# Differential probabilities turned through DRAM, in a one-layer hybrid attention kernel on one core

## The chip, the core and the metric

The kernel runs on one core of a Trainium2 chip. Five engines work side by side, each in the order of its own queue: TensorE (PE, with its weight load PEld), VectorE (DVE), ScalarE (ACT), GpSimd (POOL) and SyncE (SP), which here only issues DMAs. Engines wait for each other by semaphores. The metric is the device time of one execution in microseconds, lower is better.

## What is computed

One transformer layer over 256 latent tokens and 256 context tokens, width 2048, all in float32. A combined input projection feeds two kinds of attention: grouped-query attention (branch A, 16 heads of 128) and differential attention (branch B, 8 heads, each with two 64-wide halves). The part that the change concerns is branch B: two softmaxes are subtracted, and the difference is multiplied with the values.

```python
def diff_attn(q, k, v, lam, lam_init, subln_g):
    s = jnp.einsum('bnhid,bmhid->bhinm', q, k).astype(jnp.float32) * (dh ** -0.5)
    p = jax.nn.softmax(s, axis=-1)
    a = (p[:, :, 0] - lam * p[:, :, 1]).astype(v.dtype)
    o = jnp.einsum('bhnm,bmhe->bnhe', a, v)
    o = rms_norm(o, subln_g) * (1 - lam_init)
...
x_new = x + m_lat[2] * merge_branches(oa, ob, ga, gb, w_br_a, w_br_b, w_out)
x_new = swiglu_sublayer(x_new, ...)
```

Around it stand the modulated norms, two gates, the output projection and a gated feed-forward part with 5632 hidden columns.

## The kernel before

**Matmuls in three passes.** Each weight block of 256 rows and 512 columns is loaded by SP into a buffer `wraw` (7 of them), rounded by ACT into `whi` (L227), and the rest `wlo` is made by DVE (L229). TensorE then does three matmuls for each product: high by high, high by low, low by high (`mm3`, L233 to L235). One such block serves two row tiles of 128 tokens and two row blocks, so 12 matmuls. There are three buffers of `whi` and three of `wlo`.

**Fill pieces.** `project` (L635) runs one projection of 512 columns as a generator: each step is one weight block, 12 matmuls. `filler` (L822) chains the query groups, the gate projections and the B output projection into a stream of such pieces. Attention is cut into units that are woven into this stream: 16 units of branch B (8 heads by 2 row tiles), then 16 of branch A.

**A unit of branch B.** `front` (L713) issues six score matmuls (`s`, L734), two softmaxes (`mx` on DVE, `p` on ACT), and joins the two into one probability tile `p` of 128 queries by 512 keys (L740, L741). `back` (L746) is a generator that `on` advances by one step twice in each later unit: the tile is turned by four TensorE transposes into PSUM (`ptp`, L758) and copied by ACT to `pT` (L764); then four matmuls with the values make `o` (L779); ACT squares it, DVE scales the sum (`rstdo`, L119), POOL takes the power (L120), and DVE writes `on` (L784); two steps later `on` is turned (`otp`, L788).

**Helpers with a delay.** `after(n, fn)` runs `fn` when n weight blocks of the projections have gone by. A query group is normed by `norm_rope` (L456) for both row tiles at once, right when its projection ends, and turned 5 and 6 blocks later; its units may begin 7 blocks after the end.

**Elsewhere.** The feed-forward part already turns its activations through DRAM (`turned`, L1032): a DVE transpose within 32 by 32 blocks into `fpart`, one POOL DMA to `turn_d`, and four POOL DMAs back into `fturn`, in an order that completes the turn. In the output projection, `out_evac` (L947) makes the new rows `xn` and stores them, and `scaled` (L967) multiplies them in place by a row of scales; the call stands one block into the next column group.

**What sets the order.** The program is written in the order that these generators give. A scheduler then places the instructions on each engine's queue. `tc.issue_after(x)` keeps an instruction behind x. Buffers set the rest: the tag `p` has four tiles, `tp` and `s` two PSUM tiles each.

```python
870        pr = front(br, u)
873        on()
874        take(fill, 2)
875        on()
876        while pieces[0] + 0.5 < goal and next(fill, fill) is not fill:
877            pass
878        work.append(back(br, u, pr))
```

## Time and profile before

| What | us |
|---|---|
| Median of three runs | 1710.86 (1710.63 to 1713.24) |
| The profiled execution, whole | 1709.15 |
| Its span, first to last instruction | 1707.4 |
| TensorE busy | 1682.6 (99%) |
| VectorE busy | 1147.5 (67%) |
| ScalarE busy | 769.8 (45%) |
| GpSimd busy | 202.6 (12%) |

The granted TensorE clock is 0.998 of full speed over the span. The units of branch B lie between about 376 and 618 us, those of branch A between about 600 and 800 us, the output projection between about 890 and 985 us, and the feed-forward part behind it. In the views that follow, "x" is a count of instructions, "ns" the duration of one, and "landing" the time from the issue of a DMA until its data has arrived. Row labels read: line, engine, operation, output tile, then its inputs. L120 or L229 are lines of the kernel file as it was before.

### The profile page before, as it was taken

To read this page: it belongs to the slowest core of one execution; us is meant where nothing else is said; L and a number is where in the kernel's file an instruction comes from. 1 tells how busy PE (TensorE), PEld (TensorE's weight loads), DVE (VectorE), ACT (ScalarE), POOL (GpSimd) and SP (SyncE) were. 2 spreads that over 40 slices of the span, in tenths; PEclk is the share of its full clock that TensorE was granted. 3 is DMA by queue.
4 is the path that set the end of the run, shared out by engine and by line. 5 is a ranking of instruction groups with operands and counts; after the bars stand their busy time and mean duration, and the time that the engine had idled before them with its cause. 6 is when DMAs were issued, how large, how long until landed. Compare 5 with 4: busy or idle time off the path is not lost.

```text
span 1707.4 us, 21517 instructions
## 1 busy us (share of the span) xinstructions
PE 1682.6 (99%) x7889; PEld 1355.0 (79%) x7889; DVE 1147.5 (67%) x1459; ACT 769.8 (45%) x1045; POOL 202.6 (12%) x296
## 2 busy tenths in 40 slices
PE   6999999999999999999999999999999999999999
PEld 4677778887887788878888788888888888888887
DVE  5765779788788879796666755566666666554554
ACT  4222223245656566667544544444444444433332
POOL 1200002011031110011111101111111111100000
PEclk9999999999999999999999999999999999999999
DMA  7888785678756677777777857788888888766662
GB/s 286 304 296 279 264 333 163 216 253 260 250 181 221 218 239 242 233 239 239 246 276 237 291 173 218 227 270 269 263 268 271 263 274 258 235 219 192 218 207 90
DMA packets 181291, 413.15 MB, mean 242 GB/s; under 512 B 15008, under 2 KB 16240, under 8 KB 180928
## 3 DMA queue, kind: packets, MB, share of 16 engines
q1 hardware_dynamic: 168912, 374.23, 66.9%
q0 software_dynamic: 12272, 37.53, 7.3%
q8 instruction: 62, 1.02, 0.2%
q14 instruction: 45, 0.37, 0.1%
HBM read 395.42 MB, written 16.29 MB: 241 GB/s over the span
## 4 chain that ended last, share of the span: by engine, by line
PE 91%; DVE 5%; issue 1%; DMA 1%; ACT 1%; POOL 0%; SPq 0%; DVEq 0%; ACTq 0%; POOLq 0%
PE mm L233 28%; PE mm L234 27%; PE mm L235 27%; PE ada L290 2%; PE ptp L758 1%; DVE wlo L229 1%; PE o L779 1%; PE s L734 1%; DVE nr L479 0%; ACT whi L227 0%; DMA tok<-in_x_dram 0%; DVE ss L464 0%; DVE sq L475 0%; DVE mx L686 0%; DMA x_d<-xn 0%
## 5 line engine op out<-in xcount | busy, mean ns | idle before, releaser
L229 DVE TENSOR_TENSOR wlo<-wraw,whi 128x1024 fp32r<-128x1024 f32 x497 | 605.9, 1220 | 417.0 <-ACT whi L227 416.2
L227 ACT CAST whi<-wraw 128x1024 fp32r<-128x1024 f32 x498 | 523.3, 1052 | 745.6 <-PE mm L235 626.5
L234 PE MATMUL mm<-wlo,hT 128*128 128x512 f32 x684 | 266.4, 389 | 0.0
L235 PE MATMUL mm<-whi,hT 128*128 128x512 f32 x684 | 266.3, 389 | 0.0
L233 PE MATMUL mm<-whi,hT 128*128 128x512 f32 x684 | 266.3, 389 | 0.0
L233 PE MATMUL mm<-whi,xT 128*128 128x512 f32 x630 | 251.5, 403 | 0.7 <-ACT xT L334 0.7
L234 PE MATMUL mm<-wlo,xT 128*128 128x512 f32 x630 | 247.4, 393 | 0.9 <-DVE wlo L229 0.9
L235 PE MATMUL mm<-whi,xT 128*128 128x512 f32 x630 | 246.3, 391 | 0.0
L431 DVE SCALAR_TENSOR_TENSOR ada<-wada,vt,ada 128x1024 f32<-128x1024 f32 x120 | 152.2, 1279 | 0.0
L234 PEld LDWEIGHTS mm<-wlo,hT 128*128 128x128 f32 x684 | 128.5, 188 | 26.9 <-DVE wlo L229 0.2
L235 PEld LDWEIGHTS mm<-whi,hT 128*128 128x128 f32 x684 | 128.4, 188 | 26.8
L233 PEld LDWEIGHTS mm<-whi,hT 128*128 128x128 f32 x684 | 128.5, 188 | 26.3
L233 PEld LDWEIGHTS mm<-whi,xT 128*128 128x128 f32 x630 | 117.8, 188 | 38.1 <-issue 12.3
L234 PEld LDWEIGHTS mm<-wlo,xT 128*128 128x128 f32 x630 | 118.6, 188 | 25.9 <-DVE wlo L229 2.1
L235 PEld LDWEIGHTS mm<-whi,xT 128*128 128x128 f32 x630 | 118.3, 188 | 25.1
L233 PE MATMUL mm<-whi,fT 128*128 128x512 f32 x354 | 137.6, 389 | 0.5 <-DVE y L1077 0.5
L235 PE MATMUL mm<-whi,fT 128*128 128x512 f32 x354 | 137.4, 388 | 0.0
L234 PE MATMUL mm<-wlo,fT 128*128 128x512 f32 x354 | 137.4, 388 | 0.0
L233 PEld LDWEIGHTS mm<-whi,fT 128*128 128x128 f32 x354 | 66.5, 188 | 15.3 <-issue 0.8
L235 PEld LDWEIGHTS mm<-whi,fT 128*128 128x128 f32 x354 | 66.5, 188 | 13.7
L234 PEld LDWEIGHTS mm<-wlo,fT 128*128 128x128 f32 x354 | 66.5, 188 | 13.5
L233 PE MATMUL mm<-whi,oT 128*128 128x512 f32 x192 | 76.0, 397 | 0.0
(241 smaller groups left out, 2154.9 us busy)
## 6 DMA issues: line engine op xcount, KB each, us to landing
wraw<-in_w_in_dram SPq DMA_DIRECT2D x159, 512.0 KB, 4.8
wada<-in_w_ada_dram SPq DMA_DIRECT2D x128, 512.0 KB, 4.7
wraw<-in_w_ff_gate_dram SPq DMA_DIRECT2D x88, 512.0 KB, 4.6
wraw<-in_w_ff_up_dram SPq DMA_DIRECT2D x88, 512.0 KB, 5.2
wraw<-in_w_ff_down_dram SPq DMA_DIRECT2D x88, 512.0 KB, 4.7
wada<-in_ada_t_dram SPq DMA_DIRECT2D x64, 512.0 KB, 5.5
wraw<-in_w_br_a_dram SPq DMA_DIRECT2D x32, 512.0 KB, 5.2
wraw<-in_w_out_dram SPq DMA_DIRECT2D x32, 512.0 KB, 5.1
```

The source lines that it names most:

```text
L227: last_hi.append(nc.scalar.copy(out=hi[:, 0:nk], in_=raw[:, 0:nk]))
L229: last_lo.append((by or nc.vector).tensor_tensor(out=lo[:, 0:nk], in0=raw[:, 0:nk], in1=hi[:, 0:nk].bitcast(F32), op=ALU.subtract))
L233: nc.tensor.matmul(ps, lhsT=ah, rhs=wh, start=first, stop=False, skip_group_check=skip)
L234: nc.tensor.matmul(ps, lhsT=ah, rhs=wl, start=False, stop=False, skip_group_check=skip)
L235: return nc.tensor.matmul(ps, lhsT=al, rhs=wh, start=False, stop=last, skip_group_check=skip)
L290: last_pe[0] = nc.tensor.matmul(aps[32 * g:32 * g + 32, 0:ncol], lhsT=cst[:, k, :], rhs=rhs, start=(k < 4), stop=(k >= NKT - 4))
L431: nc.vector.scalar_tensor_tensor(out=dst, in0=wt, scalar=sc[:, 0, kt:kt + 1], in1=dst, op0=ALU.mult, op1=ALU.add)
L734: nc.tensor.matmul(sps[i], lhsT=qT[rows, x, hh, tk * P:(tk + 1) * P], rhs=kT["b", grp][y][rows, hh, :], start=(n == 0), stop=(n == 2))
L758: nc.tensor.transpose(out=tp[:, kt * P:(kt + 1) * P], in_=p[:, kt * P:(kt + 1) * P], identity=ident)
L779: nc.tensor.matmul(op[:, 0:BV], lhsT=pT[:, kt, :], rhs=vb[:, kt, hh * BV:(hh + 1) * BV], start=(kt == 0), stop=(kt == 3))
```

## The change

The differential probabilities take the way of the feed-forward activations. `turned` is split into `turn_out` (DVE transpose in blocks, one DMA to DRAM) and `turn_in` (four DMAs back), and `back` calls them for branch B: `turn_out` right at the end of the unit, `turn_in` two `on` steps later, in the middle of the next unit, and `o` two steps after that. The four TensorE transposes and the ACT copy of each unit go. `turn_in` is kept behind the newest power on POOL (`last_pow`). Beside this the second row tile of a query group is normed two blocks later than the first, the units of a group may begin 10 blocks after its projection instead of 7, and the call of `scaled` stands three blocks into the next column group instead of one.

```diff
+    def turn_out(src, n, tag="p", bufs=4):
+        part = scratch("part", tag=tag, bufs=bufs)
+        nc.vector.transpose(out=part, in_=src)
+        nc.gpsimd.dma_start(out=turn_d[n], in_=part)
+        return turn_d[n].rearrange("(a i) (k b j) -> b i k a j", a=4, k=4, b=4)
+
+    def turn_in(dst, blocks):
+        for b in range(4):
+            nc.gpsimd.dma_start(out=dst[32 * b:32 * b + 32].rearrange("p k (a j) -> p k a j", a=4), in_=blocks[b])
...
     def q_evac(qT, br):
-        def f(tk, ps):
+        def norm(tk, ps):
             o = norm_rope(ps, br, "q", tk)
...
-            after(5 + tk, turn)
+            after(5, turn)
+
+        def f(tk, ps):
+            if tk == 0:
+                norm(tk, ps)
+            else:
+                after(2, lambda: norm(tk, ps))
         return f
...
         else:
+            blocks = turn_out(pr[0], u)
+            yield None
+            yield None
             pT = scratch("pT", tag="pTb", bufs=2).rearrange("p (k c) -> p k c", k=4)
-        for i, p in enumerate(pr):
+            with tc.issue_after(last_pow[-1].ins):
+                turn_in(pT, blocks)
+            yield None
+        for i, p in enumerate(pr if br == "a" else []):
...
-            if br == "a":
-                c0 = hh % 2 * SEQ + i * P
-                split(*[x[:, :, c0:c0 + P] for x in pT], src)
-            else:
-                nc.scalar.copy(out=pT, in_=src)
...
-                after(7, lambda q=q: ready.add(q))
+                after(10, lambda q=q: ready.add(q))
...
         work.append(back(br, u, pr))
+        if br == "b":
+            next(work[-1])
...
-        next(gen)
+        take(gen, 3)
         if cg:
             for tk in range(2):
                 scaled(tk, cg - 1)
```

On GpSimd, at the first units of branch B, this is the difference of its queue. `part` and `turn_d` are the block-turned tile and its place in DRAM, `pT` the turned tile, `rstdo` the power for a unit's output.

```order
+L689 DMA turn_d<-part 128x512
+L695 DMA pT<-turn_d 32x16x32 x4
+L824 DMA gate_d<-gate 128x512 x2
+L689 DMA turn_d<-part 128x512
 L120 TENSOR_TENSOR rstdo<-rstdo,neghalf 128x1
-L802 DMA gate_d<-gate 128x512 x2
-L120 TENSOR_TENSOR rstdo<-rstdo,neghalf 128x1 x2
-L802 DMA gate_d<-gate 128x512 x2
-L120 TENSOR_TENSOR rstdo<-rstdo,neghalf 128x1 x3
-L802 DMA gate_d<-gate 128x512 x2
+L695 DMA pT<-turn_d 32x16x32 x4
+L689 DMA turn_d<-part 128x512 x2
```

The queue that held one power for each unit and two gate stores for every few now holds one store and four loads more for each unit, and the four loads of a unit stand behind the power of the unit before it.

On VectorE, in the middle of a unit of branch B, the queue reads so before the change:

```order
L229 TENSOR_TENSOR wlo<-wraw,whi 128x1024
L741 SCALAR_TENSOR_TENSOR p<-p,rs 128x512
L229 TENSOR_TENSOR wlo<-wraw,whi 128x1024
L119 TENSOR_SCALAR rstdo<-sso 128x1
L431 SCALAR_TENSOR_TENSOR ada_2768<-wada_4040,vt,ada_2768 128x1024
L784 SCALAR_TENSOR_TENSOR on<-o,rstdo,kept 128x128
```

and so with it:

```order
L761 SCALAR_TENSOR_TENSOR p<-p,rs 128x512
L431 SCALAR_TENSOR_TENSOR ada_2769<-wada_3753,vt,ada_2769 128x1024
L688 STREAM_TRANSPOSE part<-p 128x512
L229 TENSOR_TENSOR wlo<-wraw,whi 128x1024
L119 TENSOR_SCALAR rstdo<-sso 128x1
L806 SCALAR_TENSOR_TENSOR on<-o,rstdo,kept 128x128
```

One block transpose (L688) has come in between the joined probabilities and the next power's input; the rest is what it was.

On VectorE, at the start of the last column group of the output projection, the queue reads so before (`xn` are the new rows, L971 is the scaling):

```order
L956 TENSOR_TENSOR xn_7963<-xn_7963,xr 128x512
L229 TENSOR_TENSOR wlo<-wraw,whi 128x1024
L229 TENSOR_TENSOR wbig<-wraw,wbig 128x1024
L229 TENSOR_TENSOR wlo<-wraw,whi 128x1024
L971 TENSOR_TENSOR xn_7962<-xn_7962,s_8312 128x512
L971 TENSOR_TENSOR xn_7963<-xn_7963,s_8312 128x512
```

and so with the change (L995 is the same scaling):

```order
L980 TENSOR_TENSOR xn_7980<-xn_7980,xr 128x512
L229 TENSOR_TENSOR wlo<-wraw,whi 128x1024
L229 TENSOR_TENSOR wbig<-wraw,wbig 128x1024
L229 TENSOR_TENSOR wlo<-wraw,whi 128x1024
L995 TENSOR_TENSOR xn_7979<-xn_7979,s_8329 128x512
L995 TENSOR_TENSOR xn_7980<-xn_7980,s_8329 128x512
```

The call has moved in the program's text, but on this queue nothing has moved.

## The prediction

> **What bounds the kernel now.** First the busy times of the page, then its chain of waits.

> ```profile
> PE 1682.6 (99%) x7889; PEld 1355.0 (79%) x7889; DVE 1147.5 (67%) x1459; ACT 769.8 (45%) x1045; POOL 202.6 (12%) x296
> PE 91%; DVE 5%; issue 1%; DMA 1%; ACT 1%; POOL 0%; SPq 0%; DVEq 0%; ACTq 0%; POOLq 0%
> ```

> TensorE is busy 99% of the span and carries 91% of the chain. Time goes down only if TensorE does less or idles less, and up only if something new makes it idle. Then the windows, at the places where TensorE does idle. The columns are the busy time of each engine, its instructions in brackets, and at the end the clock, the DMA share and GB/s.

> ```profile
> 386.00:400.00 14.00, 13.47 (x69) 10.97 (x68) 13.29 (x20) 7.90 (x14) 1.47 (x1) 1.00 0.85 277
> 560.00:585.00 25.00, 24.17 (x122) 18.46 (x120) 22.36 (x42) 14.91 (x32) 5.25 (x5) 1.00 0.58 186
> 630.00:645.00 15.00, 14.72 (x74) 12.14 (x73) 13.57 (x26) 9.55 (x16) 2.03 (x2) 1.00 0.46 145
> 720.00:740.00 20.00, 18.07 (x82) 14.18 (x81) 19.89 (x35) 13.71 (x23) 2.04 (x2) 1.00 0.32 93
> 955.00:975.00 20.00, 18.34 (x80) 14.53 (x80) 16.26 (x19) 10.88 (x14) 3.82 (x8) 1.00 0.89 299
> ```

> The first four are stretches in which VectorE norms a query group (there it is the third number, 13.29 of 14 us and so on). TensorE idles 0.53, 0.83, 0.28 and 1.93 us in them, 3.6 us together. The fifth is the turn to the last column group of the output projection, with 1.7 us. So all that smoother norms and later row scaling can win is some 5 us.

> **Removed: the TensorE transposes.** Each of 16 units loses four.

> ```profile
> 400.82 0.96 PE L734 MATMUL s<-kbT,qT 64*128 64x512 f32 x5
> 401.71 0.66 PE L758 MATMUL ptp<-ident,p 128*128 128x128 f32 x4
> 402.12 0.48 PE L233 MATMUL mm<-whi,xT 128*128 128x512 f32 x1
> ```

> From the start of the four at 401.71 to the start of the next matmul at 402.12 pass 0.41 us. That is the price on the path, since the 0.66 us of busy time overlap the next matmul. 16 x 0.41 = 6.6 us, all of it on TensorE, so all of it is time, bar what follows.

> **Added beside the path.** Each unit gains one block transpose on VectorE and loses one ACT copy.

> ```profile
> L1035 DVE STREAM_TRANSPOSE fpart<-act x22: 669/688/704, 1027.6 to 1463.6; 128x512 f32<-128x512 f32 x22
> L764 ACT COPY pT<-ptp x16: 574/587/620, 388.2 to 599.6; 128x512 f32<-128x512 f32 x16
> 408.00:420.00 12.00, 12.00 (x66) 9.71 (x66) 9.10 (x14) 6.90 (x14) 1.47 (x1) 1.00 0.77 240
> ```

> ACT gains 16 x 0.59 = 9.4 us and VectorE does 16 x 0.69 = 11.0 us more. In a quiet stretch of units VectorE is busy 9.1 of 12 us, so 0.69 us for each unit of some 11 us hides in its idle time; in the norm stretches above there is no such cover, and up to 2 us (three units of 0.69 us) could come to light.

> **Query norms apart.** By the order, the second norm of a group still follows closely on the first; of the work that stands on VectorE between two `wlo`, a few rows have gone behind one. I take 1.0 us of the 3.6 us. The ends are 3.6 us won and 2 us lost, by the transposes just named.

> **Later row scaling.** The order on VectorE is unchanged there, so the 1.7 us stay: 0. If it did move, 1.7 us would go.

> **Added on the path: the way of one tile.** The trace of before has the same five DMAs in the feed-forward part.

> ```profile
> L1038 POOL DMA_DIRECT2D turn_d<-fpart x22: 539/562/589, 1028.6 to 1464.6; - x22
> L1041 POOL DMA_DIRECT2D fturn<-turn_d x88: 717/978/1353, 1031.3 to 1471.5; - x88
> DMA to landing us min/median/max: 2.9/5.9/8.8
> 1031.28 5.86 POOL L1041 DMA_DIRECT2D fturn<-turn_d  x8 [1.51 <-DMA turn_d<-fpart]
> ```

> The third row is that of the 88 loads. Eight issues take 5.86 us, so the fourth of a tile starts some 2.0 us after the first, and lands a median 5.9 us later: 7.9 us from first issue to a whole tile. For the fourth loads of three tiles alone:

> ```profile
> L1041 POOL DMA_DIRECT2D fturn<-turn_d x1: 968/968/968, 1033.3 to 1033.3; - x1
> DMA to landing us min/median/max: 5.2/5.2/5.2
> L1041 POOL DMA_DIRECT2D fturn<-turn_d x1: 966/966/966, 1081.0 to 1081.0; - x1
> DMA to landing us min/median/max: 6.8/6.8/6.8
> L1041 POOL DMA_DIRECT2D fturn<-turn_d x1: 963/963/963, 1165.4 to 1165.4; - x1
> DMA to landing us min/median/max: 4.6/4.6/4.6
> ```

> So 6.6 to 8.8 us.

> Now the queue decides. On POOL the four loads of unit n stand behind the power of unit n-1. That power needs the values matmul `o` of unit n-1 (then ACT's square and a VectorE scaling). And `o` of unit n waits on TensorE for the loads of unit n. This closes a **loop**: from one `o` to the next at least (o to the end of the power) + (loads landed). The first part, from the chain and from POOL's timeline:

> ```profile
> 407.97 0.89 PE o L779 x8
> ...
> 418.69 0.89 PE o L779 x8
> ...
> 432.13 0.89 PE o L779 x8
> ...
> 442.86 0.89 PE o L779 x8
> ```

> ```profile
> 409.93 1.47 POOL L120 TENSOR_TENSOR rstdo<-rstdo,neghalf 128x1 f32<-128x1 f32 x1 [3.33 <-DVE rstdo L119]
> 421.84 1.52 POOL L120 TENSOR_TENSOR rstdo<-rstdo,neghalf 128x1 f32<-128x1 f32 x1 [10.44 <-DVE rstdo L119]
> ...
> 434.10 0.56 POOL L120 TENSOR_TENSOR rstdo<-rstdo,neghalf 128x1 f32<-128x1 f32 x1
> 445.92 0.55 POOL L120 TENSOR_TENSOR rstdo<-rstdo,neghalf 128x1 f32<-128x1 f32 x1 [11.26 <-DVE rstdo L119]
> ```

> The powers end 3.43, 4.67, 2.53 and 3.61 us after their `o` starts, a mean of 3.6. The loop is 3.6 + 7.9 = **11.5 us**.

> Against it stands what TensorE has to do from one `o` to the next. Before, the steps are 10.72 us where 36 projection matmuls stand between, and 13.44 us where 48 do: 0.227 us for each matmul and 2.55 us for scores, values and transposes. Without the four transposes 2.14 us stay. In the changed order ten steps are tight (five in units 0 to 5, five in units 8 to 13), with 40, 38, 35, 43, 36 and 38, 38, 34, 36, 34 matmuls between; the mean, 37.2, gives 0.227 x 37.2 + 2.14 = **10.6 us**. The other steps are longer, since keys are made there. So TensorE waits 10 x (11.5 - 10.6) = 9 us at `o`, with all projection matmuls queued behind it. Nothing covers it. With the fourth loads' spread the loop is 3.6 + 6.6 = 10.2 to 3.6 + 8.8 = 12.4 us: 0 to 18 us.

> Other queues: SP issues nothing new. POOL's stores wait for VectorE's transpose and stand ahead of some powers (0.56 us each, inside the loop's first part). Loads ahead of a norm's power could hold VectorE for some 2.6 us (four issues), but three `wlo` buffers of 12 x 0.227 = 2.7 us each lie between that and TensorE. DMA share is 0.77 in the quiet stretch; two more 256 KB ways a unit fill most of the rest, which argues for landings no faster than in the feed-forward part.

> **The sum.** Profiled execution 1709.15 (span 1707.4, and 1.75 us around it): - 6.6 - 1.0 + 9.0 = 1710.6. The median of the runs stands 1.7 us above that execution, so the forecast is **1712.3 us**, against 1710.86.

> **Rivals.** (1) *The loads land in time.* With the loop under every step, TensorE waits for nothing: 1710.86 - 6.6 - 1.0 = 1703.3 us, and 1700.7 if all norm idling goes. For it: the least landing of the 88 is 2.9 us, which would give 3.6 + 2.0 + 2.9 = 8.5 us; from unit to unit four loads go out here, not eight. Against it: the median is 5.9.

> [...]

> (2) *A longer loop*, the slower side. If the fourth load lands 6.8 us after its issue or the power comes 4.6 us after `o`, the loop is 12.4 us and TensorE waits 18 us: 1721.3 us. It is slower than before from a loop of 11.4 us on (7.6 us of waits), by over 0.2% from 11.7 us. For it: the DMA queues are nearly full, and a store and a VectorE row came ahead of some powers. Against it: a waiting TensorE leaves ACT and VectorE idle, which shortens the first part.

> (3) *The change doesn't do all that it says*: row scaling stands where it stood, as counted above. If the norms too win nothing, the forecast is 1 us higher, 1713.3.

> **How the numbers follow.** Time = 1703.3 + 10 x (loop - 10.6). A difference of 0.2% (3.4 us) is about what this measurement can tell. Loop below 11.0 us: faster, 0.28. From 11.0 to 11.7: within 0.2%, 0.36, which holds the forecast. Above 11.7: slower, 0.36. The range runs from rival 1, a little of the norms' idling included, to rival 2 with a late transpose on top: 1702 to 1722. Faster and slower together hold more than the forecast's own case, whose range is 1707 to 1714.

> **What would show it.** `o` waiting for the loads of `pT`, in about ten units, 0 to 2 us each, and starts of `o` 11 to 12 us apart; no `ptp` in branch B; scaling rows at the same place, with the 1.7 us still lost. Wrong it is if `o` never waits (rival 1), if the wait is longer than 1.2 us a unit (rival 2), or if TensorE idles at a norm or elsewhere for POOL.

## The result, and the profile after

| | before | changed |
|---|---|---|
| median of four runs | 1710.74 us (1710.37 to 1713.24) | 1727.77 us (1724.25 to 1729.1) |
| profiled execution, its span | 1709.15, 1707.4 us | 1729.1, 1727.2 us |
| mean granted TensorE clock | 0.998 | 0.991 |

The changed kernel is slower: ratio 1.0098, 95% interval 1.0086 to 1.011. That is 17 us, where the forecast was 1.5 us and the range ended at 1722. The profiled execution is the slowest of the four; their mean clocks are 0.991 to 0.995. The busy times of its page, and the shares of its chain by engine:

```profile
PE 1686.7 (98%) x7825; PEld 1356.2 (79%) x7825; DVE 1157.8 (67%) x1475; ACT 761.8 (44%) x1029; POOL 258.1 (15%) x376
PE 84%; DVE 5%; issue 4%; DMA 3%; POOL 2%; ACT 2%; SPq 0%; POOLq 0%; DVEq 0%; ACTq 0%
```

The 64 transposes are gone (x7889 is now x7825), yet TensorE is busy 4 us longer, and its share of the chain fell from 91% to 84%. Both need explaining: TensorE waits more, and what it does takes longer. By windows of 100 us, first the kernel before, then the changed one (after the length of the window: busy PE, PEld, DVE, ACT, POOL; clock; DMA share; GB/s):

```profile
400.00:500.00 100.00, 100.00 (x501) 80.52 (x501) 78.56 (x122) 61.32 (x109) 19.46 (x21) 1.00 0.73 234
500.00:600.00 100.00, 98.34 (x495) 77.39 (x495) 87.36 (x144) 60.23 (x113) 18.58 (x18) 1.00 0.68 218
600.00:700.00 100.00, 99.72 (x483) 81.96 (x482) 86.07 (x125) 64.27 (x107) 8.38 (x10) 1.00 0.72 240
```

```profile
400.00:500.00 100.00, 92.93 (x436) 73.23 (x435) 77.13 (x120) 51.47 (x93) 44.20 (x55) 0.97 0.85 259
500.00:600.00 100.00, 91.23 (x428) 70.74 (x427) 83.87 (x143) 55.46 (x102) 39.48 (x49) 0.96 0.73 215
600.00:700.00 100.00, 96.03 (x448) 78.62 (x447) 78.06 (x106) 53.29 (x89) 14.80 (x19) 0.95 0.80 259
```

TensorE idles 7 to 9 us in each of the first two, and the clock is no longer 1.00. The idle time stands where it was predicted, at `o`. First the group of its matmuls in the kernel before and in the changed one (busy, mean ns, then the idle time before them and what ended it), then two of the waits in TensorE's timeline, and on POOL what stands before the loads of unit 3:

```profile
L779 PE MATMUL o<-vb,pT 128*128 128x128 f32 x128 | 17.2, 278 | 0.7 <-DVE kaT L239 0.7
L801 PE MATMUL o<-vb,pT 128*128 128x128 f32 x128 | 20.6, 312 | 16.3 <-DMA pT<-turn_d 13.2 <-DVE wlo L229 3.1
```

```profile
421.25 2.02 PE L801 MATMUL o<-vb,pT 128*128 128x128 f32 x8 [2.46 <-DMA pT<-turn_d]
447.90 1.43 PE L801 MATMUL o<-vb,pT 128*128 128x128 f32 x8 [3.87 <-DMA pT<-turn_d]
```

```profile
436.21 1.53 POOL L120 TENSOR_TENSOR rstdo<-rstdo,neghalf 128x1 f32<-128x1 f32 x1 [0.62 <-DVE rstdo L119]
437.70 2.91 POOL L695 DMA_DIRECT2D pT<-turn_d  x4
```

The loads start as the power ends (436.21 + 1.53 = 437.74), and `o` at 447.90 waits for the last of them: the loop is there. (The 3.1 us put down to `wlo` are the wait of unit 15, which ends at 643.77; the last of its loads landed at 643.52, so I count them to the loop too.)

What was not predicted stands right behind the waits. Windows of 3.41 us in TensorE's rows, each with its busy time and, at the end, clock, DMA share and GB/s; every second one follows the one above it:

```profile
417.87:421.28 3.41, 0.95 (x5) 1.00 1.01 290
421.28:424.69 3.41, 3.41 (x12) 0.50 0.90 301
445.18:448.59 3.41, 0.69 (x6) 1.00 0.91 272
448.59:452.00 3.41, 3.41 (x11) 0.50 0.77 284
550.99:554.40 3.41, 1.06 (x9) 1.00 1.00 357
554.40:557.81 3.41, 3.41 (x10) 0.50 1.01 380
595.37:598.78 3.41, 1.58 (x8) 1.00 0.88 255
598.78:602.19 3.41, 3.41 (x10) 0.50 0.94 221
```

In these rows, after a window in which TensorE is busy only 0.69 to 1.58 of 3.41 us, it runs 3.41 us at half clock (0.50): a matmul of 512 columns starts every 0.43 us there, against every 0.23 us at full clock. There are six such stretches (the others start at 578.29, and at 643.15 for 6.83 us), 23.9 us in all, of which TensorE is busy 23.2; taken as half of that, an estimate, the half clock costs 11.6 us. Five follow a wait at `o`; the one at 598.78 follows a wait of 1.83 us for `wlo`. The kernel before has none between 29 and 1700 us: its longest wait in that time is 1.56 us. The 11.6 us are those of the profiled execution; by their mean clocks, 0.003 to 0.007 below that of the kernel before, the four executions lost an estimated 5 to 12 us.

So, from profile to profile: - 6.6 us of transposes + 16.3 us of waits at `o` + 11.6 us of half clock = + 21.3; the spans differ by 19.8. The other 1.5 us are won in the rest; between 720 and 760 us, where the query norms crowded, TensorE idles 2.0 us less.

### The profile page after: what moved, and what is told of

It is laid out like the page before. It is cut to its first block, busy times and chain, and to the rows that moved or that the text cites. A ratio compares the mean times of both kernels' runs of the same rounds, so it can differ in the third digit from the quotient of the medians.

```text
span 1727.2 us, 21532 instructions
## 1 busy us (share of the span) xinstructions
PE 1686.7 (98%) x7825; PEld 1356.2 (79%) x7825; DVE 1157.8 (67%) x1475; ACT 761.8 (44%) x1029; POOL 258.1 (15%) x376
## 4 chain that ended last, share of the span: by engine, by line
PE 84%; DVE 5%; issue 4%; DMA 3%; POOL 2%; ACT 2%; SPq 0%; POOLq 0%; DVEq 0%; ACTq 0%
PE mm L233 26%; PE mm L234 25%; PE mm L235 25%; PE ada L290 2%; DMA pT<-turn_d 2%; DVE wlo L229 1%; POOL pT L695 1%; ACT whi L227 1%; PE o L801 1%; POOL rstdo L120 1%; DVE mx L700 0%; ACT p L703 0%; PE ptp L784 0%; DMA tok<-in_x_dram 0%; DMA gate_d<-gate 0%
## 5 line engine op out<-in xcount | busy, mean ns | idle before, releaser
L233 PE MATMUL mm<-whi,hT 128*128 128x512 f32 x684 | 266.1, 389 | 0.0
L233 PE MATMUL mm<-whi,xT 128*128 128x512 f32 x630 | 254.6, 407 | 0.7 <-ACT xT L334 0.7
L235 PE MATMUL mm<-whi,xT 128*128 128x512 f32 x630 | 249.7, 396 | 0.0
L233 PEld LDWEIGHTS mm<-whi,xT 128*128 128x128 f32 x630 | 119.8, 191 | 43.8 <-issue 16.1
L233 PEld LDWEIGHTS mm<-whi,hT 128*128 128x128 f32 x684 | 128.4, 188 | 26.7
L235 PEld LDWEIGHTS mm<-whi,xT 128*128 128x128 f32 x630 | 120.6, 191 | 25.7
L233 PE MATMUL mm<-whi,fT 128*128 128x512 f32 x354 | 137.5, 388 | 0.5 <-DVE y L1094 0.5
L689 POOL DMA_DIRECT2D turn_d<-part x38 | 22.8, 601 | 429.9 <-DVE part L688 429.7
L233 PEld LDWEIGHTS mm<-whi,fT 128*128 128x128 f32 x354 | 66.4, 188 | 15.3 <-issue 0.8
```

The lines of the kernel that those rows point to most:

```text
L233: nc.tensor.matmul(ps, lhsT=ah, rhs=wh, start=first, stop=False, skip_group_check=skip)
L235: return nc.tensor.matmul(ps, lhsT=al, rhs=wh, start=False, stop=last, skip_group_check=skip)
L689: nc.gpsimd.dma_start(out=turn_d[n], in_=part)
```

## The experiments

Theory A is the account above: the loop through POOL's queue makes TensorE wait at `o`, and each long wait costs again by the clock. Its rivals: the traffic and POOL time of the way through DRAM as such (B), the other two parts of the change (C), and a clock that costs nothing of its own (D). Ratios are to the kernel before on the same chip, with their 95% intervals.

### The order behind the power taken away

```diff
-            with tc.issue_after(last_pow[-1].ins):
-                turn_in(pT, blocks)
+            turn_in(pT, blocks)
```

> The changed kernel, but the four loads of a unit are no longer ordered behind the power of the unit before; on POOL they now stand directly behind the unit's own store. Theory A (the loop: loads behind the previous power, TensorE waits at o, and after a long wait runs 3.41 us at half clock): no loop, so o waits less than 1 us in every unit, the clock is 1.00 from 400 to 600 us, and the time is about 1703 to 1706 us. Rival B (the way through DRAM itself, by its traffic and by POOL's issue time, holds up loads and powers wherever they stand): o still waits 2 us or more in several units and the time stays above 1720 us. A result between means that POOL, now waiting for the store's landing ahead of a power, delays something else: look for rstdo or rstd at the end of a wait.

Measured 1714.72 us against 1710.06: 1.0029 (1.0018 to 1.0039). Some 12 of the 17 us went with one line, so B is not the account of most of the loss. But it is not 1703 to 1706: theory A alone missed by 9 us. In its trace (of the fastest of its eight executions, 1711.34 us) the waits at `o` fell to 3.2 us, still over 1 us in two units, one stretch at half clock is left (3.41 us at 0.50 from 583.48 us), and there are waits of another kind. POOL, then TensorE:

```profile
474.57 0.72 POOL L695 DMA_DIRECT2D pT<-turn_d  x1 [3.38 <-DMA turn_d<-part]
475.31 1.67 POOL L120 TENSOR_TENSOR rstd<-rstd,neghalf 128x8 f32<-128x8 f32 x1
```

```profile
478.90 0.50 PE L234 MATMUL mm<-wlo,xT 128*128 128x512 f32 x1 [1.86 <-DVE wlo L229]
```

A load that stands directly behind its own store waits 3.38 us here for the store to land, and the power of a key norm stands behind it on POOL; VectorE waits for that power, and `wlo`, behind it on VectorE, comes late. Call this A': a load that waits on POOL holds the powers behind it. How much of the 9 us it makes is not shown by this run.

### The other two parts alone

```diff
-            blocks = turn_out(pr[0], u)
...
+                nc.scalar.copy(out=pT, in_=src)
```

> Only the other two parts of the change (query norms apart, later row scaling); branch B's probabilities are turned on TensorE as before. Theory A: all of the loss comes from the way through DRAM, so this is 0 to 3 us below the kernel before: 1708 to 1711 us. Rival C (the norms apart, or the scaling, cost the time): above 1715 us. In the window 720 to 760 us TensorE's waits should fall from 3.5 to about 0.5 us, as in the changed kernel.

Measured 1709.22 us: 0.9994 (0.9986 to 1.0003), 0.8 us less, which is not clear of noise. C falls: norms and scaling together cost nothing, and give about what was predicted.

### The way through DRAM alone

```diff
-                after(10, lambda q=q: ready.add(q))
+                after(7, lambda q=q: ready.add(q))
...
-        take(gen, 3)
+        next(gen)
```

(and the query norms as before.)

> Only the way through DRAM; norms and row scaling as before. Theory A: as slow as the changed kernel or up to 3 us slower, 1726 to 1731 us, with waits of 2 to 4 us at o in every second unit and stretches of half clock behind them. Rival C: near 1710 us or below.

Measured 1726.11 us: 1.0092 (1.0078 to 1.0105). The whole loss is in this part. Its trace has 10.6 us of waits at `o` and three stretches at half clock (the clock is 0.98 in each of the three windows of 100 us from 400 us on). From 40 to 1700 us TensorE idles 14.2 us more than before; with an estimated 5.1 us for the clock and without the 6.6 us of the transposes that makes 12.7 of the 16.5 us between the two spans, and the rest is not accounted for. The trace tells more of the clock. It waits 2.43 us at `o` (the first row) without a slow stretch behind it, and 2.13 us at branch A's transposes (the second) with one:

```profile
578.61 1.13 PE L795 MATMUL o<-vb,pT 128*128 128x128 f32 x8 [2.43 <-DMA pT<-turn_d]
...
624.57 0.73 PE L778 MATMUL ptp<-ident,p 128*128 128x128 f32 x4 [2.13 <-DVE on L800]
```

```profile
573.79:577.21 3.42, 2.39 (x11) 1.58 (x10) 2.33 (x6) 2.54 (x6) 0.00 (x0) 1.00 0.99 229
577.21:580.62 3.41, 2.01 (x13) 1.86 (x14) 1.89 (x3) 0.56 (x3) 0.79 (x2) 1.00 1.04 347
580.62:584.03 3.41, 3.41 (x18) 2.31 (x17) 2.69 (x6) 2.14 (x3) 2.70 (x5) 1.00 0.61 195
621.61:625.02 3.41, 1.28 (x11) 0.95 (x9) 2.95 (x5) 1.06 (x2) 2.48 (x4) 1.00 1.05 377
625.02:628.43 3.41, 3.41 (x10) 2.72 (x9) 3.24 (x7) 3.03 (x7) 2.00 (x3) 0.50 1.01 293
```

The windows are laid out in steps of 3.413 us from the slow stretch at 625.02. The longer wait falls into two of them, in which TensorE is busy 2.39 and 2.01 us, and the clock stays at 1.00; the shorter one lies within one, with 1.28 us busy, and the next is at 0.50. So in these rows the clock doesn't go by the length of a wait: it falls behind the window with the least busy time.

### TensorE kept busy in the same waits

```diff
+        if u in (1, 3, 9, 11, 15):
+            for _ in range(22):
+                nc.tensor.transpose(out=op[:, 0:P], in_=ident, identity=ident)
```

> The changed kernel with 22 transposes of the identity (about 2.3 us) put on TensorE ahead of o in units 1, 3, 9, 11 and 15, those that wait 2.5 to 4 us. They fill the wait with work that has no use, so the waiting itself costs what it did. Theory A with the clock as a cost of its own: the idle time left is under 2 us in each of the five, four or five of the stretches at half clock (3.41 us each, so 1.7 us lost in each, 3.4 us in the last) go, and the time falls by 6 to 9 us to 1719 to 1722 us. Rival D (the lower clock in the records costs nothing of its own; only the wait does): the same as the changed kernel, 1727 to 1730 us. If the transposes come too early and only add work: above 1730 us.

Measured 1718.4 us: 1.0046 (1.0033 to 1.006), 9.4 us less than the changed kernel (8.9 by the ratios), for 110 more transposes: a little more than the 6 to 9 us expected. No stretch at half clock is left (the clock is 1.00 from 400 to 700 us), the one behind the wait for `wlo` included; the waits at `o` are still there, 6.2 us as idle time and the rest filled:

```profile
L804 PE MATMUL o<-vb,pT 128*128 128x128 f32 x128 | 17.4, 279 | 6.2 <-DMA pT<-turn_d 6.2
L802 PE MATMUL o<-ident 128*128 128x128 f32 x110 | 12.8, 273 | 0.0
```

6.2 + 12.8 us is no less than the 16.3 us of waits in the changed kernel. So what fell is the clock's own cost, some 9 us, beside the 11.6 us worked out from one trace: D falls.

### `o` later, and the loads of four kinds

With `o` half a unit later, the loads stand in program order behind the power of the unit before the last, and the loop spans two units:

```diff
             with tc.issue_after(last_pow[-1].ins):
                 turn_in(pT, blocks)
             yield None
+            yield None
```

> The changed kernel with o half a unit later, so that in program order a unit's loads stand behind the power of the unit before the last: the loop is still there but spans two units (some 21 us of TensorE work against 12 to 14 us). Theory A: no wait over 1 us at o, no stretch at half clock that follows one, and about 1704 to 1708 us; some loads may again stand on POOL waiting for their store ahead of a power, as in e1_no_order, which would cost 1 to 4 us at wlo. Rival B (traffic and POOL time of the DRAM way as such): above 1715 us.

Measured 1709.68 us: 0.9993 (0.9984 to 1.0002). No wait at `o` at all (expected; second row), and 18 us less than the changed kernel: the loop is what cost them. But it ends 1.7 us above the expected range, and 7 us above 1703. TensorE waits 4.9 us for `wlo` (first row); 2.47 us of that end at 484.15, and a stretch at half clock (0.98 over 400 to 500 us), which costs an estimated 1.7 us, stands behind them. A' is there too. On POOL (last row) the loads of unit 6 had waited 8.55 us for their store, with the power of a key norm behind them, and TensorE waits 1.73 us for what that power scales. That A' is all of the rest is not shown, and the kernel with both later, below, speaks against it:

```profile
L234 PE MATMUL mm<-wlo,xT 128*128 128x512 f32 x302 | 119.4, 395 | 4.9 <-DVE wlo L229 4.9
L802 PE MATMUL o<-vb,pT 128*128 128x128 f32 x128 | 17.5, 278 | 0.0
```

```profile
471.52 2.99 POOL L695 DMA_DIRECT2D pT<-turn_d  x4 [8.55 <-DMA turn_d<-part]
```

The same without the order on the power (the two edits above together):

> As e5_late_o, but the loads stand directly behind their store on POOL as in e1_no_order. This splits what e1_no_order still lost: its waits at o (1.21, 1.65 and 0.35 us) should go, its waits behind a power of a norm (2.1 us at 476 us, 1.9 us at 580 us and the half clock behind it) should stay. Theory A': powers held on POOL by a load that waits for its store: 1709 to 1713 us, slower than e5_late_o by 3 us or more. If it is the same as e5_late_o within 2 us, the powers held on POOL are not what e1_no_order lost.

Measured 1719.4 us: 1.0052 (1.0039 to 1.0065), 9.7 us above the one with the order. The direction is that of A', the size was missed, since the powers of `o` itself came late too. One started only at 425.32 us: the load ahead of it started at 424.64, after POOL had idled 7.64 us (the row puts the wait down to `s`; that it was for the load's own store, issued at 416.13, is my inference). TensorE waited 2.54 us for what that power scales (last row). It ran 17.1 us at half clock behind this and other waits (the clock is 0.97 over 400 to 500 us and 0.95 over 500 to 600), which costs an estimated 8.5 us, against 1.7 us with the order: 6.8 of the 9.7 us.

```profile
424.64 0.71 POOL L695 DMA_DIRECT2D pT<-turn_d  x1 [7.64 <-PE s L754]
425.32 0.62 POOL L120 TENSOR_TENSOR rstdo<-rstdo,neghalf 128x1 f32<-128x1 f32 x1
```

```profile
426.47 0.34 PE L810 MATMUL otp<-ident,on 128*128 128x128 f32 x1 [2.54 <-DVE on L806]
```

Then the loads on other queues, ACT's and SP's (`nc.scalar` and `nc.sync`), in place of POOL's, without the order and with `o` where the changed kernel has it; first the edit for ACT (`turn_in` is given the queue):

```diff
-            with tc.issue_after(last_pow[-1].ins):
-                turn_in(pT, blocks)
+            turn_in(pT, blocks, nc.scalar)
```

> The loads of a unit issued by ACT in place of POOL, with no order on a power; POOL is left with the stores and the powers. Theory A': no loop and no held power, so 1703 to 1708 us, if ACT's own rows behind a waiting load (casts of the weights, exponentials) are not late: ACT is busy about half of the time there. A load that waits on ACT for its store for 2 us or more would show as whi late and TensorE waiting for weights: then 1710 us or more. POOL's busy time in 400 to 500 us falls from 44 us to some 25 us.

> The loads of a unit issued by SP, in line with the loads of the weights. Theory A': no loop, no held power: 1703 to 1708 us, if a weight load queued behind them is not late for TensorE. If the loads, behind weight loads that wait for a free buffer, come late, o waits: above 1715 us.

Measured 1744.89 us (1.0199, 1.0184 to 1.0213) and 1737.93 us (1.0163, 1.0149 to 1.0178): both in the time of the second branch of what was expected, but each with the waits of the other, and slower than the changed kernel. TensorE's idle time, first with the loads on ACT, then on SP:

```profile
L800 PE MATMUL o<-vb,pT 128*128 128x128 f32 x120 | 19.8, 305 | 18.1 <-DMA pT<-turn_d 14.1 <-issue 3.1 <-ACT o L810 0.7
```

```profile
L234 PE MATMUL mm<-wlo,xT 128*128 128x512 f32 x274 | 111.7, 408 | 7.7 <-DVE wlo L229 7.7
L233 PE MATMUL mm<-whi,xT 128*128 128x512 f32 x273 | 108.7, 408 | 4.8 <-ACT whi L227 4.8
```

On ACT the loads stand among exponentials, casts and the square of the `o` before, and come late: 18.1 us at `o`, where a wait for weights was expected (2.4 us for `whi`). On SP, where a wait at `o` was expected, little is left there (2.1 us); the weights' own loads stand behind those of `pT`, and both halves of the weights come late. The half clock costs an estimated 13.7 us with the loads on ACT (0.93, 0.97 and 0.97 in the windows of 100 us from 400 us on) and 6.8 us with those on SP (0.95, 1.00 and 0.98). In both, the in-order queue passes the waiting on to what stands behind it.

### Loads and `o` both later

```diff
             blocks = turn_out(pr[0], u)
             yield None
             yield None
+            yield None
...
                 turn_in(pT, blocks)
             yield None
+            yield None
```

> The changed kernel with loads half a unit later and o a whole unit later. The loads stand behind the power of the unit before the last, so that the loop spans two units as in e5_late_o, and their store has 11 us or more to land, so that no load should hold POOL ahead of a power. Theory A with A': what e5_late_o still lost at wlo (2.6, 1.9 and 1.1 us and 1.7 us by half clock) goes, no wait at o over 0.5 us, and the time is 1702 to 1706 us, below the kernel before by 0.2% or more. If it stays at 1708 us or above, the rest of the loss isn't POOL's waiting for stores but the DMA traffic or POOL's own issue time.

Measured 1708.63 us against 1709.79: 1.0000 (0.9991 to 1.0009), not the 1702 to 1706 expected. No wait at `o`, no half clock (1.00 from 400 to 1000 us), and still the 6.6 us of the transposes don't show. Nor is it A': only the loads of units 0, 1, 2 and 9 still wait on POOL for their store, and VectorE waits for POOL's powers 10.5 us between 390 and 660 us (11.0 in the kernel before, 20.4 with `o` later alone), yet TensorE's wait for `wlo` is what it was. A window of the crowded stretch, in this kernel and then in the next one below:

```profile
560.00:585.00 25.00, 22.16 (x108) 16.87 (x107) 23.62 (x44) 14.12 (x29) 13.29 (x15) 1.00 0.81 249
```

```profile
560.00:585.00 25.00, 23.50 (x129) 18.18 (x128) 21.99 (x45) 15.25 (x33) 7.64 (x6) 1.00 0.71 201
```

(before: 24.17 us of TensorE and 22.36 us of VectorE.) The first row has VectorE busy 23.62 of 25 us and TensorE idle 2.84 us, 2 us more than before. Over 390 to 660 us it waits 4.8 us for `wlo` (first row), where the kernel before waits 0.9 (second), and once 2.4 us at branch A's transposes (for a VectorE row, `on`), where that one doesn't wait:

```profile
L234 PE MATMUL mm<-wlo,xT 128*128 128x512 f32 x305 | 119.7, 393 | 4.8 <-DVE wlo L229 4.8
```

```profile
L234 PE MATMUL mm<-wlo,xT 128*128 128x512 f32 x305 | 119.4, 391 | 0.9 <-DVE wlo L229 0.9
```

Three accounts are left: VectorE's added transposes, POOL's issue time, or the traffic of the way through DRAM.

### The crowded units turned on TensorE

```diff
+        elif u in TE:
+            yield None
+            pT = scratch("pT", tag="pTb", bufs=2).rearrange("p (k c) -> p k c", k=4)
+            tp = tp_ps("ptp")
...
+            nc.scalar.copy(out=pT, in_=tp.rearrange("p (k q) -> p k q", k=4))
         else:
             blocks = turn_out(pr[0], u)
```

with `TE = (8, 12, 13, 14)`, and `(7, 8, 11, 12, 13, 14)` in a second kernel.

> As e9_late_both, but units 8, 12, 13 and 14, whose stores fall into the stretches in which VectorE norms query groups, are turned on TensorE as before. e9_late_both never waited at o and still gained nothing measurable; its trace waits some 5.5 us more at wlo than the kernel before (513 to 524 and 574 to 580 us), with VectorE busy 23.6 of 25 us in 560 to 585 us. Theory V (VectorE's added transposes, 0.69 us a unit, come to light in those stretches): 12 units win 12 x 0.41 = 4.9 us, the waits at wlo shrink by 2 to 5 us: 1704 to 1707 us. Rival (POOL's issue time ahead of the norms' powers, or the DMA traffic of the other units): wlo waits as in e9_late_both and, with four units' transposes back on TensorE (1.6 us), 1709 to 1711 us.

> As e10_mix4, with units 7 and 11 turned on TensorE too. By theory V the stretches are wholly as in the kernel before, and 10 units win 4.1 us: 1704 to 1707 us, within 1 us of e10_mix4. By the rival 1709 to 1711 us.

Measured 1705.08 us (0.9968, 0.9956 to 0.9981) and 1706.46 us (0.9977, 0.9966 to 0.9987) against 1709.99. Both are faster than the kernel before, by 4.9 and 3.5 us, and the first beats the changed kernel by 1.3%. They lie 1.4 us apart, where within 1 us was expected; their intervals overlap. The wait for `wlo` fell from 4.8 to 1.5 us, and the one at branch A's transposes is gone:

```profile
L234 PE MATMUL mm<-wlo,xT 128*128 128x512 f32 x309 | 121.3, 392 | 1.5 <-DVE wlo L229 1.5
```

Without their way through DRAM these four units take both the transposes from VectorE and the loads from POOL (13.29 to 7.64 us in the stretch above). So the runs show that the loss sat in these units. That it is VectorE's row is argued from the traces, and not separated by a run: in 505 to 525 and 560 to 585 us together VectorE is busy 42.5 us in the kernel with both later, and 40.9 us in the one before and in the mix of four. Its waits for POOL's powers there are 1.9 us in the first of these, but 2.8 us in the mix, which has lost the wait for `wlo`; and for `whi`, which late weights would hold up, it waits 0.4 us or less in both.

## Why the prediction was wrong, step by step

- **The bound.** Right as far as the traces go: TensorE's work, its waits and its clock account for the time of the kernel before and of the changed one.
- **The transposes, - 6.6 us.** About right in size, though not measured alone: where 12 of 16 units go through DRAM and little else waits (the mix of four), 12 x 0.41 = 4.9 us less 0.6 us of added idle time would be 4.3, and the spans differ by 4.1. The measured gain of 4.9 us has the other two parts in it, so that it equals 12 x 0.41 is chance.
- **The norms, - 1.0 us, and the scaling, 0.** The two alone gave 0.8 us, not clear of noise. But the scaling seems to do a little: the idle time at the turn of the column group, 1.7 us before, is 0.6 us in the changed kernel (first row, the stretch some 18 us later), 0.6 us for `wlo` with the other two parts alone (and 0.7 us a little later), and 1.8 us with the way through DRAM alone, where the scaling stands as before. The order on VectorE is the same, but VectorE waits there for the store of `xn` 0.86 and 1.11 us before, and 0.80 us in the changed kernel: a wait that the prediction did not look for. The last norm stretch, which idled 1.93 us, idles no more (second row).

```profile
973.00:995.00 22.00, 21.40 (x94) 17.07 (x93) 17.63 (x20) 12.50 (x16) 3.92 (x8) 1.00 0.91 301
```

```profile
735.00:760.00 25.00, 25.00 (x120) 20.76 (x119) 22.40 (x31) 14.89 (x24) 2.03 (x2) 1.00 0.89 326
```

- **VectorE's transposes hidden.** Only by the loop: a TensorE that waits leaves VectorE idle (it is busy 18.73 of 25 us in 560 to 585 us of the changed kernel). With the loop gone, as in the kernel with both later, TensorE waits 3.9 us more for `wlo` than before, about twice the 2 us that the prediction gave as an upper end; that the transposes are the cause is argued above.
- **The loop, + 9 us.** The mechanism was right, and so was the mean. This is one of the two steps that failed, by how the mean was used. "10 x (loop - 10.6)" lets a short loop pay for a long one, and on TensorE it can't. From one `o` to the landing of the next unit's last load, and the wait, in the ten steps named:

| unit | 1 | 2 | 3 | 4 | 5 | 9 | 10 | 11 | 12 | 13 |
|---|---|---|---|---|---|---|---|---|---|---|
| loop, us | 13.7 | 9.9 | 13.9 | 7.3 | 10.7 | 14.9 | 10.4 | 12.4 | 8.6 | 11.5 |
| wait, us | 2.46 | 0 | 3.87 | 0 | 0.30 | 4.05 | 0 | 2.54 | 0 | 0 |

The mean is 11.3 us, against 11.5 predicted. But what the long loops have over 10.6 us adds up to 13.5 us, if the short ones give nothing back, and the waits are 13.2 us, all in odd units. Unit 15, which was not counted as tight, waits 3.1 us more: 16.3 us for 9. The bounds, too, were made of means (every step at 10.2 or at 12.4 us). From the first load's issue to the last landing, in units 2, 3, 4 and 9, 11, 12:

```profile
425.41:431.20 5.79, 5.79 (x28) 4.25 (x28) 4.42 (x7) 3.09 (x5) 2.91 (x5) 1.00 0.79 214
437.70:447.66 9.96, 6.33 (x29) 4.84 (x27) 7.98 (x12) 4.12 (x8) 3.51 (x6) 1.00 0.91 253
450.53:455.23 4.70, 4.70 (x19) 3.56 (x19) 2.23 (x3) 1.24 (x2) 2.89 (x5) 0.84 0.43 124
543.44:553.21 9.77, 5.85 (x27) 4.44 (x25) 7.29 (x11) 5.29 (x10) 4.55 (x8) 1.00 0.97 278
569.03:578.24 9.21, 6.80 (x33) 4.98 (x29) 7.71 (x12) 5.13 (x9) 3.37 (x6) 1.00 1.00 282
581.62:586.95 5.33, 5.33 (x26) 3.84 (x25) 4.29 (x11) 3.03 (x6) 3.91 (x6) 0.99 0.26 62
```

From the first load's issue, the last landing takes 8.9 to 10.0 us in units 1, 3, 9 and 11, where the DMA engines are full (share 0.91 to 1.02), and 4.7 to 5.8 us in units 2, 4 and 12, where they aren't (0.26 to 0.79). Units 5, 10 and 13 lie between, 7.1 to 7.9 us, with full engines too (0.91 to 0.97), so the share is not the whole account. The 7.9 us taken was the middle of a wide spread. Why long and short landings alternate with the units was not tried.
- **The clock, not in the sum at all.** This is the other step that failed, and the larger: the sum prices a microsecond of wait at a microsecond of time. The half clock behind the waits cost an estimated 11.6 us by the trace, some 9 us by the kernel that keeps TensorE busy. Without it the time would lie within the range. The prediction's own rival of a longer loop had 18 us of waits, near the 16.3 measured, and gave 1721.3 us, because it too priced a wait at its length.
- **The rivals.** That the loads land in time (1703.3 us) falls with the landings above. The longer loop came nearest, and by the prediction's own sign (more than 1.2 us a unit) it holds: 13.2 us in the ten steps are 1.3 us each. But the mean loop was not longer; its spread was.

With the two terms as that trace has them: 1709.15 - 6.6 - 1.0 + 16.3 + 11.6 = 1729.5 us, against 1729.1 in the profiled execution.

## What to carry to other kernels

Where an engine waits for a loop with spread in it, sum the positive parts step by step; a mean near the bound hides most of the wait. In the changed kernel six windows of 3.41 us in which TensorE was busy only 0.69 to 1.58 us were each followed by half clock, which cost an estimated 1.7 us more (once 3.1 us): price long waits with that. Check an asynchronous way not only for when its data land but for what stands behind each of its waiting issues on an in-order queue. Taking work from the bounding engine pays only where the engines that get it have room: the best version here left the crowded units as they were.

## What the runs showed of the hardware

One of these loads held ACT's queue 0.56 us at the least when ACT issued it, and POOL's 0.70 us when POOL did, in the changed kernel:

```profile
L695 ACTq DMA_DIRECT2D pT<-turn_d x64: 564/565/1597, 398.6 to 642.9; - x64
```

```profile
L695 POOL DMA_DIRECT2D pT<-turn_d x64: 698/789/968, 397.7 to 635.9; - x64
```
